# Value products in plain F32 in two 64-column array tiles, and latent scores with keys on partitions and the shift as a contraction row

## The chip, the core and the metric

The kernel runs on one core of a Trainium2 chip. The metric is the device time of one execution in microseconds; the profiled execution is one such execution with every instruction's start and duration recorded.

## What is computed

One layer of a hybrid trunk over 1024 latent tokens and 256 context tokens, width 1024, all in F32: half a SwiGLU step, then two attentions beside each other on one normalised input, their gated merge, and another half SwiGLU step. The change lies in the two attentions, both with 8 heads and values of width 64:

```python
# neighbourhood attention, by row of the 64-wide grid and block of 16 columns
s_loc = einsum('bjqhd,bjakhd->bhjqak', q_r, k_b) + bias; s_loc = where(valid, s_loc, neg)
s_ctx = einsum('bjqhd,bkhd->bhjqk', q_r, k_ctx)
p = softmax(concatenate([s_loc, s_ctx], -1), -1)
o_na = einsum(p_loc, v_b) + einsum(p_ctx, v_ctx)
# multi-head latent attention: 96 query/key dimensions, 1024 + 256 keys
s = einsum('bqhd,bkhd->bhqk', q * 96 ** -0.5, k)
o_mla = einsum('bhqk,bkhd->bqhd', softmax(s, -1), v)
```

## The kernel before

F32 products are made from FP32R halves: an operand x is split into hi (x rounded to FP32R) and lo (the rest), and `mm3` adds hi·hi, hi·lo and lo·hi. Nearly all of TensorE's work is such matmuls. The attentions lie between about 1342 and 1746 us of the profiled execution.

Neighbourhood attention has 32 items, one for each head and block of 16 columns, with 256 queries in two sets of 128. For each set the scores of 384 local keys and 256 context keys stand with queries on partitions; VectorE adds the bias and takes the row maximum (L1817), copies the context scores with their maximum (L1792), and ScalarE takes exp with the negated maximum as bias and the row sum beside it (L1826). Then TensorE transposes the weights 128x128 at a time (`turned`, L157), ScalarE casts them from PSUM to FP32R (L1850) and VectorE subtracts to get the rest (L1851). `weigh` multiplies each with a value tile of 128 columns, of which 64 are the values' hi and 64 their lo, so that two matmuls of 256 columns give all four products; the two halves are added afterwards. Six value blocks an item are twelve such matmuls.

Latent attention has 32 items of 256 queries, four for each head. `MlaItem.scores` makes scores of 1024 latent and 256 context keys for two sets of 128 queries, queries on partitions, again with three FP32R matmuls. The rest is as above: copy with maximum, exp (L1928), reciprocal of the sum (L1932), then five parts, each with four transposes, a cast (L1954), a subtraction (L1955) and four value matmuls of 256 columns.

`head_out` ends an item of both: it adds the two halves (ScalarE copies L1764 to L1768, VectorE L1769), multiplies with the reciprocal of the row sum (GpSimd L1770), and writes hi and lo of the result (L1772, L1773). The reciprocals come by `wide`: GpSimd spreads the sums over 128 columns (L1784) and TensorE transposes that, a pair for every two items.

The order is written out by hand: inside these stages `pin` keeps every instruction in program order on its engine. While item n is weighed, the scores of item n + 3 are made (`AHEAD`), value products run two parts late (`LAG`), and exp and sums are dealt out from the list `soft`. A matmul's records carry the helper's line (`mmul` L154, `turn_` L157, engine helpers L120, loads L132), so they are told apart by tiles: PSUM banks `bs` (scores, three), `bm` (transposes, three) and `bv` (outputs, two); `w` are weight tiles with queries, keys and values, `xu` and `t` work tiles, `st` small statistics, `xo` the outputs. Loads and stores all go through SyncE's queue (SP). The last items of latent attention are filled with `FirstMerge`, the first products of the merge.

Of the kernel before, what the change touches and what calls it, by code (L numbers as in the profile page):

```python
# [15 lines left out]
P = 128  # L16
# [27 lines left out]
def hybrid_block(ctx: ExitStack, tc: tile.TileContext, a: dict, out: bass.AP):  # L44
# [31 lines left out]
    def T2(dt=F32, n=512):  # L76
        return pools["t"].tile([P, n], dt, tag="t", name=nm("t"))

# [1295 lines left out]
    vws = [DR([NH, P, 512]) for _ in range(4)]  # L1374
    vcs = DR([NH, P, 256])
# [53 lines left out]
    def va_tile(s, t):  # L1429
        pb = s.product(t)  # L1430
        v = U(F32R)
        vv = v.rearrange("p (h c) -> p h c", h=NH)
        pv = pb.rearrange("p (h c) -> p h c", h=NH)
        split_to(vv[:, :, 0:64], vv[:, :, 64:128], pv)
        if t < 8:
            for j in range(4):
                for r in range(2):
                    row = 2 * t + r
                    o, q = 64 * r + KSTART[j], (row % 4) * 32
                    g = (row // 4) * P  # L1440
                    store(vws[j][:, q:q + 32, g:g + P].rearrange("h p c -> p h c"),
                          f32(v[o:o + 32, :]).rearrange("p (h c) -> p h c", h=NH))
        else:
            g = (t - 8) * P
            store(vcs[:, :, g:g + P].rearrange("h p c -> p h c"), f32(v).rearrange("p (h c) -> p h c", h=NH))
# [76 lines left out]
    vs = DR([NLAT + NCTX, D])  # L1522
# [46 lines left out]
    class NaHead:  # L1569


        def loads(self, h):
# [11 lines left out]
            self.bias = [U() if h == 1 else W(F32)]  # L1584
            ld(self.bias[0][:, :768], a["bias"][h, 0])
            yield
            if h == 1:
                self.second_bias()
                yield
            self.va = va = W()  # L1590
            for j in range(2):
                self.values(va, j)
            yield
            ld(f32(kvc[:, 256:512]), vcs[h])
            if h != 1:
                self.second_bias()
            yield
            if h == 0:
                self.third_bias()
                yield  # L1600
            self.vb = vb = W()
            for j in range(2, 4):
                self.values(vb, j)
            yield
            if h:
                self.third_bias()
                yield

        def second_bias(self):
            self.bias.append(W(F32))  # L1610
            ld(self.bias[1][:, :768], a["bias"][self.h, 1])

        def third_bias(self):
            self.bias.append(U(F32, "y") if self.h else W(F32))
            ld(self.bias[2][:, :768], a["bias"][self.h, 2])

        def values(self, v, j):
            o = (j % 2) * 512
            ld(f32(v[:, o:o + 512]), vws[j][self.h])
# [33 lines left out]
    def kv_heads(ci, cn):  # L1653
# [8 lines left out]
        for i, t in enumerate(tiles_of(ci)):  # L1662
            v = U(F32R)
# [707 lines left out]
```

## Time and profile before

| | |
|---|---|
| median of 3 runs | 2550.99 us (2550.88 to 2553.09) |
| span of the profiled execution | 2549.3 us |
| TensorE matmul busy | 2524.4 us, 99% |
| TensorE weight loads busy | 2156.4 us, 85% |
| VectorE busy | 1936.7 us, 76% |
| ScalarE busy | 1259.6 us, 49% |
| GpSimd busy | 214.1 us, 8% |
| neighbourhood attention, 1342 to 1480 us | PE 135.50, VectorE 128.13, ScalarE 120.16, GpSimd 61.59 us busy |
| latent attention, 1480 to 1746 us | PE 264.24, VectorE 221.09, ScalarE 210.21, GpSimd 68.96 us busy |

PE is TensorE's matmuls, PEld its weight loads, DVE is VectorE, ACT ScalarE, POOL GpSimd. Matmuls are pipelined, so the time of one is read from start to start and not from its own duration. A row of groups reads: line, engine, operation, output<-input tiles, shapes, count, then busy time and mean duration in ns, then idle time before and what ended it.

### The profile page before, as it was taken

How to read it: one execution, taken by the hardware profiler on the slowest of the kernel's cores; microseconds unless marked ns; L12 is line 12 of the kernel's file. 1: busy time of each engine (PE TensorE's matmuls, PEld its weight loads, DVE VectorE, ACT ScalarE, POOL GpSimd, SP SyncE). 2: the span in 40 equal slices, each digit the busy share in tenths (PEclk: the TensorE clock that was granted, in tenths of full speed). 3: DMA queues.
4: the chain of work that ended last, by engine and by line, in shares of the span. 5: the costliest groups of instructions: out<-in, count | busy, mean ns of one | idle time of the engine just before them, and what ended most of it. 6: DMA issues, size and time to landing. Idle time of an engine off the chain costs nothing.

```text
span 2549.3 us, 38224 instructions
## 1 busy us (share of the span) xinstructions
PE 2524.4 (99%) x13416; PEld 2156.4 (85%) x13416; DVE 1936.7 (76%) x3629; ACT 1259.6 (49%) x2375; POOL 214.1 (8%) x372
## 2 busy tenths in 40 slices
PE   8999999999999999999999999999999999999998
PEld 6888888888998888889889999998888888888887
DVE  4789986887786577874568988887886888766777
ACT  6632223446654753433448987783366323233444
POOL 1000000001000000001003522221021000000002
PEclk9999999999999999999999999999999999999999
DMA  8555543943674666755978733206845445326724
GB/s 308 162 174 196 192 153 116 346 137 132 230 271 141 211 235 221 244 180 179 297 292 289 236 92 75 65 13 245 320 135 201 160 158 166 112 99 239 269 71 165
DMA packets 245760, 479.47 MB, mean 188 GB/s; under 512 B 30464, under 2 KB 71616, under 8 KB 245568
## 3 DMA queue, kind: packets, MB, share of 16 engines
q1 hardware_dynamic: 245568, 477.02, 55.6%
q8 instruction: 106, 1.74, 0.3%
q14 instruction: 86, 0.70, 0.1%
HBM read 348.93 MB, written 127.99 MB: 187 GB/s over the span
## 4 chain that ended last, share of the span: by engine, by line
PE 85%; ACT 6%; DVE 6%; issue 3%; DMA 1%; POOL 0%; SPq 0%; DVEq 0%; POOLq 0%; ACTq 0%
PE bs L154 36%; PE bm L154 27%; PE bv L154 19%; PE bm L157 2%; ACT xu L1928 2%; DVE xu L1792 2%; DVE t L1955 1%; ACT t L1954 1%; ACT t L120 1%; PE bs L157 1%; DVE xv L120 1%; DVE xu L120 1%; ACT t L1928 1%; ACT t L1768 0%; ACT xu L120 0%
## 5 line engine op out<-in xcount | busy, mean ns | idle before, releaser
L120 ACT CAST xu<-t 128x512 fp32r<-128x512 f32 (+1 forms) x270 | 160.9, 601 | 494.2 <-DVE t L120 352.3
L154 PE MATMUL bm<-xu,xu 128*128 128x512 f32 (+2 forms) x1572 | 366.6, 386 | 0.0
L154 PE MATMUL bs<-xv,xu 128*128 128x512 f32 x1488 | 357.3, 389 | 0.3 <-DVE t L120 0.3
L154 PEld LDWEIGHTS bm<-xu,xu 128*128 128x128 f32 x1572 | 288.1, 188 | 56.7 <-ACT t L120 0.2
L154 PE MATMUL bv<-xv,xu 128*128 128x512 f32 x1342 | 335.4, 389 | 0.0
L154 PEld LDWEIGHTS bs<-xv,xu 128*128 128x128 f32 x1488 | 279.1, 188 | 59.0 <-issue 1.1
L154 PEld LDWEIGHTS bv<-xv,xu 128*128 128x128 f32 x1342 | 251.8, 188 | 52.2
L154 PE MATMUL bs<-xv,xv 128*128 128x512 f32 x1086 | 265.8, 390 | 0.0
L120 DVE TENSOR_TENSOR xu<-xu,xu 128x512 fp32r<-128x512 f32 (+1 forms) x296 | 202.2, 688 | 54.0 <-ACT xu L120 53.6
L154 PEld LDWEIGHTS bs<-xv,xv 128*128 128x128 f32 x1086 | 203.0, 188 | 41.7
L154 PE MATMUL bs<-xu,xu 128*128 128x512 f32 (+1 forms) x972 | 226.2, 382 | 0.0
L120 DVE TENSOR_TENSOR t<-t,t 128x512 f32<-128x512 f32 (+2 forms) x278 | 185.3, 674 | 45.2 <-ACT t L120 36.1
L154 PE MATMUL bs<-w,w 96*128 96x512 f32 (+3 forms) x832 | 206.1, 366 | 1.6 <-DVE st L1817 1.3
L154 PEld LDWEIGHTS bs<-xu,xu 128*128 128x128 f32 x972 | 177.4, 188 | 35.7 <-issue 1.4
L120 ACT CAST xv<-t 128x512 fp32r<-128x512 f32 x170 | 105.8, 622 | 167.4 <-PE bm L154 69.3
L120 POOL TENSOR_SCALAR st<-st 128x1 f32<-128x1 f32 (+1 forms) x66 | 29.7, 450 | 1884.8 <-ACT t L120 1866.7
L120 DVE TENSOR_TENSOR xu<-t,xu 128x512 fp32r<-128x512 f32 (+1 forms) x270 | 179.3, 664 | 10.7 <-ACT xu L120 10.6
L154 PE MATMUL bm<-xv,xv 128*128 128x512 f32 x690 | 182.9, 390 | 0.0
L120 ACT CAST xu<-xu 128x512 fp32r<-128x512 f32 x218 | 132.6, 618 | 70.2 <-DMA xu<-in_wo 46.8
L120 DVE TENSOR_TENSOR xv<-t,xv 128x512 fp32r<-128x512 f32 x170 | 117.1, 689 | 65.5 <-ACT xv L120 65.1
L154 PE MATMUL bv<-t,w 128*128 128x256 f32 x896 | 150.0, 288 | 2.5 <-DVE t L1955 1.6
L154 PEld LDWEIGHTS bm<-xv,xv 128*128 128x128 f32 x690 | 129.2, 188 | 27.0 <-issue 0.4
(246 smaller groups left out, 4228.1 us busy)
## 6 DMA issues: line engine op xcount, KB each, us to landing
d<-t SPq DMA_DIRECT2D x366, 256.0 KB, 2.7
t<-d SPq DMA_DIRECT2D x274, 256.0 KB, 3.7
xu<-in_f1w SPq DMA_DIRECT2D x59, 512.0 KB, 4.2
xu<-in_f2w SPq DMA_DIRECT2D x58, 512.0 KB, 3.8
t<-in_wada SPq DMA_DIRECT2D x112, 256.0 KB, 5.0
xv<-in_f1w SPq DMA_DIRECT2D x44, 512.0 KB, 6.8
xu<-in_winT SPq DMA_DIRECT2D x38, 512.0 KB, 5.2
w<-d SPq DMA_DIRECT2D x32, 512.0 KB, 6.6
```

The source lines that it names most:

```text
L120: return lambda *x, **y: pin(f(*x, **y))
L154: return pin(nc.tensor.matmul(o, s, m, start=start, stop=stop, skip_group_check=open_group[0]))
L157: return pin(nc.tensor.transpose(o, x, i))
L1792: nc.vector.tensor_scalar(dst, src, 1.0, FMIN, op0=ALU.mult, op1=ALU.max, accum_out=m)
L1928: nc.scalar.activation(x, x, AF.Exp, bias=n_[:, s:s + 1], accum_out=l[:, i:i + 1])
L1954: nc.scalar.copy(t[0], pb)
L1955: nc.vector.tensor_tensor(t[1], pb, f32(t[0]), op=ALU.subtract)
```

## The change

**Value products.** Values and weights stay plain F32 and are not split. `weigh` now makes two matmuls: values of 64 columns stand once in the left and once in the right 64 columns of the array, each with its own half of the queries, and the output fills 128 PSUM partitions. In the neighbourhood items the two sets of queries are the two tiles, 128 columns each; an item's transposed weights are copied out of PSUM once (two copies on ScalarE, one on VectorE) and its five pairs of products are collected and run together (`NaItem.weigh`). `NaPair` holds the output of two items and ends both together.

**Latent attention.** It has 16 items of 512 queries. `maxima` makes hi·hi scores with queries on partitions, ten blocks ("top") an item, only for the maximum. `shift` takes their maximum and negates it on VectorE; `row` transposes it to a row and writes it by four DMAs into partition 96 of the queries' tile, against a row of ones in the keys' tile. `scores` then makes scores with keys on partitions, for a block of 128 keys and 512 queries, in three matmuls of which the first contracts 97 rows, and exp goes from PSUM straight into the weights (`X`, a tile of five blocks). There are no transposes of weights. The row sums come from GpSimd's additions of blocks 0 to 4 (`add`), VectorE's reduction over blocks 5 to 9 and an addition (`total`), and a matmul with ones that sums over partitions and spreads the sum; `out` takes the reciprocal of 128x256 in PSUM and the product. `follow` sets the order: of item i's ten key blocks, the first half is weighed after the seventh, the second half and the ones after the third block of the next item, and the output follows two blocks later.

Loads and stores of values halve, since no lo is kept.

Diff, cut to its core; the bodies that fall away are in the listing above:

```diff
+    def X():
+        return pools["x"].tile([P, 2560], F32, tag="x", name=nm("xp"))
...
     def va_tile(s, t):
         pb = s.product(t)
-        v = U(F32R)
-        vv = v.rearrange("p (h c) -> p h c", h=NH)
-        pv = pb.rearrange("p (h c) -> p h c", h=NH)
-        split_to(vv[:, :, 0:64], vv[:, :, 64:128], pv)
+        v = U()[:, :512]
+        act.copy(v, pb)
...
-    def head_out(pv, n, h, hi, lo, shape):
...
-        x = sums[n // 2].rearrange("p (x i o) -> p i x o", i=2, o=1).to_broadcast([P, 2, 2, 64])
-        nc.gpsimd.tensor_copy(wide(n).rearrange("p (i x c) -> p i x c", i=2, x=2), x)
+        x = sums[n // 2].rearrange("p (x o) -> p x o", o=1).to_broadcast([P, 4, 64])
+        nc.gpsimd.tensor_copy(wide(n).rearrange("p (x c) -> p x c", x=4), x)
...
+    def weigh(pv, c, vts, pts, start, stop):
+        open_group[0] = True
+        for e in range(2):
+            n = pts[e].shape[-1]
+            mmul(pv[64 * e:64 * e + 64, c:c + n], vts[e], pts[e], start, stop)
+        open_group[0] = False
...
-    def weigh(pv, vtile, pt, start, stop):
-        mmul(pv[:, :256], vtile, pt[0], start=start, stop=False)
-        mmul(pv[:, :256], vtile, pt[1], start=False, stop=stop)
...
+        def out(self, n, h, j):
+            pv, t = self.pv[0], T2()
+            rb, o = t[:, 0:256], t[:, 256:512]
+            for i in range(2):
+                turn_(pv[:, 256 + i * P:256 + (i + 1) * P], wide(n)[:, i * P:(i + 1) * P], ident)
+            nc.scalar.copy(rb, pv[:, 256:512])
+            for x in range(len(self.pv)):
+                c = slice(x * P, x * P + 256 // len(self.pv))
...
+        def weigh(self, last=True):
+            pv = na_pairs[self.n // 2].bank(self.n)
+            for i, (vts, t) in enumerate(self.jobs):
+                weigh(pv, (self.n % 2) * P, vts, (t[:, 0:P], t[:, P:2 * P]), not self.begun, last and i == len(self.jobs) - 1)
+                self.begun = True
+            self.jobs = []
...
-                nc.scalar.copy(oh, src)
-                nc.vector.tensor_tensor(ol, src, f32(oh), op=ALU.subtract)
+                (nc.scalar.copy if eng else nc.vector.tensor_copy)(t[:, :n], pb[:, :n])
...
+        def maxima(self):
+            hd = self.hd
+            self.m, self.mc = m, mc = ST(8), ST(4)
+            q = lambda t: hd.qh[:QK, self.c0 + t * P:self.c0 + (t + 1) * P]
+            def top(d, c, pb):
+                nc.vector.tensor_reduce(d[:, c:c + pb.shape[-2]], pb, axis=AX.X, op=ALU.max)
+            for t in range(4):
                 for e in range(2):
...
+                    pb = PB("m")
+                    mmul(pb, q(t), hd.kh[:QK, e * 512:(e + 1) * 512], True, True)
+                    top(m, 2 * t + e, pb.rearrange("p (o c) -> p o c", o=1))
+                    yield
+                if t % 2:
+                    pb = PB("m")
                     for x in range(2):
...
+                        mmul(pb[:, x * 256:(x + 1) * 256], q(t - 1 + x), hd.kvc[:QK, 0:256], True, True)
+                    top(mc, t - 1, pb.rearrange("p (o c) -> p o c", o=2))
+                    yield
+        def shift(self):
+            n_, u = ST(4), ST(4)
+            nc.vector.tensor_reduce(u, self.m.rearrange("p (t e) -> p t e", t=4), axis=AX.X, op=ALU.max)
+            nc.vector.tensor_tensor(u, u, self.mc, op=ALU.max)
+            nc.vector.tensor_scalar(n_, u, -1.0, None, op0=ALU.mult)
+            self.n_ = n_
+        def row(self):
+            pt = PB("m")
+            turn_(pt[:4, :P], self.n_, ident)
+            rows = kr.rearrange("p a b -> p (a b)")[0:4, (self.i % 2) * P:(self.i % 2) * P + P]
+            nc.vector.tensor_copy(rows, pt[:4, :P])
+            for t in range(4):
+                put(f32(self.hd.qh[QK:QK + 1, self.c0 + t * P:self.c0 + (t + 1) * P]), rows[t:t + 1, :])
+        def scores(self, kb):
+            hd, c = self.hd, slice(self.c0, self.c0 + 512)
+            hi, lo = hd.key(0, kb), hd.key(1, kb)
+            pb = PB("s")
+            mmul(pb, hi[:QK + 1, :], hd.qh[:QK + 1, c], True, False)
+            mmul(pb, hi[:QK, :], hd.ql[:QK, c], False, False)
+            mmul(pb, lo[:QK, :], hd.qh[:QK, c], False, True)
+            if kb % 5 == 0:
+                self.pt[kb // 5] = X()
+            nc.scalar.activation(self.part(kb), pb, AF.Exp)
+        def part(self, kb):
+            return self.pt[kb // 5][:, (kb % 5) * 512:(kb % 5) * 512 + 512]
+        def add(self, kb):
+            if kb == 1:
+                self.acc = T2()
+            nc.gpsimd.tensor_tensor(self.acc, self.part(0) if kb == 1 else self.acc, self.part(kb), op=ALU.add)
+        def total(self):
+            self.l = T2()
+            nc.vector.tensor_reduce(self.l, self.pt[1].rearrange("p (k q) -> p q k", k=5), axis=AX.X, op=ALU.add)
+            nc.vector.tensor_tensor(self.l, self.l, self.acc, op=ALU.add)
+        def weigh(self, half):
+            if half == 0:
+                self.pv = PB("v")
+            for kb in range(5 * half, 5 * half + 5):
+                v = self.hd.v[:, kb * 64:(kb + 1) * 64]
+                x = self.part(kb)
+                weigh(self.pv, 0, (v, v), (x[:, 0:256], x[:, 256:512]), kb == 0, kb == 9)
+            if half:
+                v = ones.to_broadcast([P, 64])
+                weigh(self.pv, 256, (v, v), (self.l[:, 0:256], self.l[:, 256:512]), True, True)
+        def out(self):
+            t, h, pv = T2(), self.hd.h, self.pv
+            rb, o = t[:, 0:256], t[:, 256:512]
+            nc.vector.reciprocal(rb, pv[:, 256:512])
+            nc.vector.tensor_tensor(o, pv[:, 0:256], rb, op=ALU.mult)
+            def views(s):
+                hi, lo = [x[:, self.c0 + s * 256:self.c0 + s * 256 + 256] for x in omla[h // 2]]
+                return hi, lo, lambda x: x
+            heads_out(o, rb, (h % 2) * 64, views)
...
+    def follow(i, kb):
+        prev = mla[i - 1] if i else None
+        item = mla[i] if i < len(mla) else None
+        after = mla[i + 1] if i + 1 < len(mla) else None
+        if kb == 0 and prev:
+            prev.total()
+        if kb == 0 and i % 2 == 0 and i // 2 + 1 < NH:
+            mla_heads[i // 2 + 1].second()
+        if kb == 2 and prev:
+            prev.weigh(1)
+        if kb == 4 and prev:
+            prev.out()
+        if item and 1 <= kb < 6:
+            item.add(kb) if kb < 5 else None
+        if after and kb == 5:
+            after.shift()
+        if kb == 5 and i % 2 and i // 2 + 2 < NH:
+            mla_heads[i // 2 + 2].first()
+        if after and kb == 6:
+            after.row()
+        if item and kb == 6:
+            item.weigh(0)
+    for i, item in enumerate(mla):
+        for kb in range(10):
+            item.scores(kb)
+            next(tops, None)
+            if i == 0:
+                finish_one()
+                if pending and kb % 2 == 0:
+                    ending += pending.pop(0)
+            follow(i, kb)
...
```

In the orders below each row is an instruction: line, operation, output<-inputs and shape, then the engines whose work it waits for. First TensorE in the middle of the latent attention, before: scores of one item (`bs`), value products of an earlier one (`bv`) and transposes (`bm`) take turns, part by part.

```order
L157 MATMUL bm_18104<-ident,t_17652 128x128 [waits PE_49]
L157 MATMUL bm_18104<-ident,t_17652 128x128 x3
L154 MATMUL bs_18116<-w_17997,w_17995 128x512 [waits DVE_49]
L154 MATMUL bs_18116<-w_17998,w_17995 128x512
L154 MATMUL bs_18116<-w_17997,w_17996 128x512
L154 MATMUL bv_18080<-t_18070,w_17509 128x256 [waits Activation_49]
L154 MATMUL bv_18080<-t_18071,w_17509 128x256 [waits DVE_49]
L154 MATMUL bv_18080<-t_18070,w_17509 128x256
L154 MATMUL bv_18080<-t_18071,w_17509 128x256
```

And now, at the seventh key block of an item: a score block, a top block (`bm` from `w`), the transpose of the shift (`bm` from `ident` and `st`), and the first half of the value products as one burst.

```order
L157 MATMUL bs_3246_16099<-w_3106_15493,w_3107_15494 128x512 [waits Activation_49]
L157 MATMUL bs_3246_16099<-w_3109_15496,w_3107_15494 128x512
L157 MATMUL bs_3246_16099<-w_3106_15493,w_3124_15572 128x512
L157 MATMUL bm_3247_16104<-w_3175_15789,w_3174_15788 128x512 [waits DVE_49]
L160 MATMUL bm_3248_16107<-ident_76,st_3240_16078 4x128 [waits DVE_49,PE_49]
L157 MATMUL bv_3249_16114<-xp_3222_16001,w_3125_15573 64x256 x8
L157 MATMUL bv_3249_16114<-xp_3222_16001,w_3125_15573 64x256 [waits Activation_49]
L157 MATMUL bv_3249_16114<-xp_3222_16001,w_3125_15573 64x256
L157 MATMUL bs_3250_16125<-w_3106_15493,w_3107_15494 128x512
```

The transposes of weights are gone from between the scores, the value products stand together, and a transpose that waits for VectorE's shift has come in ahead of them. On VectorE a stretch of a latent item, before: copies with maximum from `bs`, subtractions from `bm`, and the small sums.

```order
L1955 TENSOR_TENSOR t_16111<-bm_16105,t_16110 128x512 [waits Activation_49]
L1792 TENSOR_SCALAR xu_16061,st_16056<-bs_16135 128x512 [waits PE_49]
L1955 TENSOR_TENSOR t_16131<-bm_16125,t_16130 128x512 [waits Activation_49]
L1931 TENSOR_TENSOR st_15804<-st_15924 128x2
L1955 TENSOR_TENSOR t_16150<-bm_16144,t_16149 128x512 [waits Activation_49,Pool_49]
L1932 RECIPROCAL st_15804<-st_15804 128x2 [waits DVE_49]
L1792 TENSOR_SCALAR xu_16061,st_16056<-bs_16156 128x512 [waits PE_49]
L1924 TENSOR_REDUCE st_16057<-st_16056 128x2 [waits DVE_49]
```

And now, in two pieces, first from the total of the item before to its reciprocal (`st` from `bm` are top reductions).

```order
L1993 TENSOR_REDUCE t_16749<-xp_16661 128x512 [waits Activation_49]
L1938 TENSOR_REDUCE st_16663<-bm_16746 128x1 [waits PE_49]
L1994 TENSOR_TENSOR t_16749<-t_16749,t_16607 128x512 [waits DVE_49,Pool_49]
L1938 TENSOR_REDUCE st_16663<-bm_16762 128x1 [waits PE_49]
L1938 TENSOR_REDUCE st_16663<-bm_16772 128x1 [waits PE_49]
L2010 RECIPROCAL t_16806<-bv_16704 128x256 [waits PE_49]
```

The subtractions and copies are gone; the total and the reciprocal stand among the top reductions. The second piece of the same engine, two top reductions later, goes from the product to the copy of the row.

```order
L2011 TENSOR_TENSOR t_16806<-bv_16704,t_16806 128x256 [waits DVE_49]
L1938 TENSOR_REDUCE st_16821<-bm_16823 128x1 [waits PE_49]
L1957 TENSOR_REDUCE st_16827<-st_16663 128x4 [waits DVE_49]
L1938 TENSOR_REDUCE st_16821<-bm_16836 128x1 [waits PE_49]
L1958 TENSOR_TENSOR st_16827<-st_16827,st_16664 128x4 [waits DVE_49]
L1959 TENSOR_SCALAR st_16826<-st_16827 128x4 [waits DVE_49]
L1966 COPY kr<-bm_16839 4x128 [waits DMAHW6_49,DMAHW1_49,DMAHW7_49,DMAHW0_49,PE_49]
```

A 128x512 reduction (the total), a 128x256 reciprocal and ten top reductions have taken the place of the subtractions and the copies with maximum; one top reduction (the seventh's) stands between the first and the second step of the shift. Third, TensorE in the neighbourhood attention, before: two value blocks of four matmuls, with transposes and scores between.

```order
L154 MATMUL bv_14928<-t_14839,w_14560 128x256
L154 MATMUL bv_14928<-t_14840,w_14560 128x256
L154 MATMUL bv_14928<-t_14839,w_14560 128x256
L154 MATMUL bv_14928<-t_14840,w_14560 128x256
L157 MATMUL bm_14935<-ident,xu_14711 128x128
L157 MATMUL bm_14935<-ident,xu_14712 128x128
L157 MATMUL bm_14935<-ident,xu_14711 128x128
L157 MATMUL bm_14935<-ident,xu_14712 128x128
L154 MATMUL bs_14943<-w_14851,w_14849 128x256
```

And now, where an item's value products come after the scores and ahead of the last two transposes:

```order
L157 MATMUL bs_13978<-w_13775,w_13769 128x384 [waits DVE_49]
L157 MATMUL bs_13978<-w_13775,w_13770 128x384
L157 MATMUL bv_13934<-t_13897,w_13527 64x128 [waits DMAHW3_49]
L157 MATMUL bv_13934<-t_13897,w_13527 64x128 x3
L157 MATMUL bv_13934<-t_13917,w_13519 64x128 x4
L157 MATMUL bv_13934<-t_13945,w_13527 64x128 [waits Activation_49]
L157 MATMUL bv_13934<-t_13945,w_13527 64x128
L160 MATMUL bm_13998<-ident,xp_13790 128x128 [waits PE_49]
L160 MATMUL bm_13998<-ident,xp_13790 128x128
```

Three groups of four matmuls between transposes and scores have become one burst of ten.

More of the change, by code (lines that the diff above doesn't have):

```diff
@@ L1750, in weights @@
         open_pool("w", "weights", 16, "left")
[L1752 to L1775 removed]
+    sums = {}
     def wide(n):
@@ L1798, in hybrid_block @@
+    na_pairs = [NaPair() for _ in range(NH * 2)]
     class NaItem:
```

336 lines of the change are left out of this document (142 added, 194 removed).

## The prediction

> **What bounds the kernel now.** I read the busy times first, then the chain that ended last.
>
> ```profile
> span 2549.3 us, 38224 instructions
> PE 2524.4 (99%) x13416; PEld 2156.4 (85%) x13416; DVE 1936.7 (76%) x3629; ACT 1259.6 (49%) x2375; POOL 214.1 (8%) x372
> PE 85%; ACT 6%; DVE 6%; issue 3%; DMA 1%; POOL 0%; SPq 0%; DVEq 0%; POOLq 0%; ACTq 0%
> ```
>
> TensorE is busy 99% and carries 85% of the chain, so what the change takes from TensorE's stream is gain and what makes TensorE wait is loss. The profiled execution spans 2549.3 us, 1.7 us under the median of 2550.99; I carry the differences over to the median. Then the stretches of the change, by windows (busy time of each engine, then granted clock, DMA share and GB/s):
>
> ```profile
> 1300.00:1342.00 42.00, 42.00 (x246) 37.03 (x245) 23.09 (x66) 15.13 (x28) 0.99 (x5) 1.00 0.68 247
> 1420.00:1460.00 40.00, 39.84 (x318) 39.26 (x317) 39.07 (x142) 37.84 (x93) 20.93 (x36) 1.00 0.75 222
> 1480.00:1746.00 266.00, 264.24 (x1870) 243.11 (x1869) 221.09 (x640) 210.21 (x471) 68.96 (x118) 1.00 0.24 61
> ```
>
> The neighbourhood attention (the middle row, typical of 1342 to 1480) has PE, VectorE and ScalarE all nearly full; the latent attention (the last row) has PE full at 99% and VectorE at 83%. The clock is whole. Now one latent item of 256 queries, by the timeline of PE (start, duration of the group, count):
>
> ```profile
> 1600.08 0.60 PE L157 MATMUL bm<-ident,xu 128*128 128x128 f32 x4
> 1600.44 0.94 PE L154 MATMUL bs<-w,w 96*128 96x512 f32 x3
> 1601.22 0.64 PE L154 MATMUL bv<-t,w 128*128 128x256 f32 x4
> 1601.70 0.60 PE L157 MATMUL bm<-ident,t 128*128 128x128 f32 x4
> ...
> 1606.57 0.38 PE L157 MATMUL bv<-ident,rope 128*128 128x128 f32 x2
> ...
> 1608.40 0.60 PE L157 MATMUL bm<-ident,xu 128*128 128x128 f32 x4
> ```
>
> A part is four transposes (0.36 from start to start), three score matmuls (0.78) and four value matmuls (0.48). Five parts take 1608.40 − 1600.08 = 8.32 us, that is 16.64 us for 512 queries; nothing stands idle between them. Only starts count: a matmul's own duration overlaps the next.
>
> **The prices of what is added.** A plain F32 matmul shows as two passes; the trace has such matmuls already, in four 32-column tiles that run side by side:
>
> ```profile
> 41.81 1.82 PE L154 MATMUL bv<-xv,sc 128*32 128x128 f32 x60
> 806.17 1.29 PE L154 MATMUL bv<-t,xu 128*128 128x512 f32 x5
> 807.40 1.07 PE L154 MATMUL bm<-t,strip 128*32 128x256 f32 x16
> 808.40 0.98 PE L154 MATMUL bv<-t,xu 128*128 128x512 f32 x3
> 1300.66 3.56 PE L154 MATMUL bm<-xu,xu 128*128 128x512 f32 x15
> L154 PE MATMUL bv<-xv,sc x256: 272/273/423, 10.7 to 43.4; 128*32 128x128 f32 x128
> L154 PE MATMUL bv<-t,w 128*128 128x256 f32 x429 | 71.5, 285 | 1.0 <-DVE t L1955 0.9
> L154 PE MATMUL bs<-xv,xu 128*128 128x512 f32 x1488 | 357.3, 389 | 0.3 <-DVE t L120 0.3
> L157 PEld LDWEIGHTS bv<-ident,rope x64: 137/141/143, 1354.2 to 1737.8; 128*128 128x128 f32 x64
> ```
>
> 60 records in four tiles are 15 passes of 128 columns: (1.82 − 0.27)/14 = 0.11 us a pass, so 0.22 for 256 columns, the four tiles sharing it. An ordinary 512-column matmul starts every (3.56 − 0.39)/14 = 0.23, one of 256 every (0.64 − 0.28)/3 = 0.12 (the four at 1601.22). The burst at 807.40 costs more than its four passes: the five before it need 4 x 0.23 = 0.92 to their last start, and 1.23 pass until the burst, 0.08 over a normal 0.23; the burst lasts 1.00 against 0.88; the three behind it have starts (0.98 − 0.39)/2 = 0.295 apart, 0.13 lost. I price a change of tile shape and back at 0.33 us. The Trainium skill ("TensorEngine Tiling (Array Packing)", Key Properties) says that changing the tiling mode drains TensorE; these rows agree.
>
> **The latent attention, 16 items of 512 queries.** Removed for each: 40 transposes, 40 value matmuls, one pair of wide transposes. Added: ten "top" blocks of hi·hi scores for the maxima (8 of 512 columns, 4 of 256: 8 x 0.23 + 4 x 0.12 = 2.32), 10 x 3 score matmuls of 512 (6.90), one small transpose for the row (0.11), 20 value matmuls in two 64-column tiles, which are ten pairs of two passes (20 x 0.22 = 4.40), the sum by ones (0.44), and two bursts (0.66). Sum 14.83 against 16.64: −1.81 an item if TensorE never waits, −29 us over 16.
>
> But it will wait. In VectorE's order the reduction of the seventh top block stands between the shift's first and last steps, and TensorE turns the row right behind that top block's matmul. The durations, by groups of the latent stretch and of single tiles:
>
> ```profile
> L1792 DVE TENSOR_SCALAR_CACHE_REDUCE xu<-bs 128x512 f32<-128x512 f32 x87 | 57.5, 680 | 0.0
> L1931 DVE TENSOR_TENSOR st<-st 128x2 f32<-128x2 f32 x22 | 3.4, 153 | 0.0
> L1824 DVE TENSOR_REDUCE st<-st 128x2 f32<-128x4 f32 x16 | 2.4, 149 | 0.2
> L1932 DVE RECIPROCAL st<-st 128x2 f32<-128x2 f32 x21 | 3.3, 155 | 0.0
> L1769 DVE TENSOR_TENSOR t<-t,bv 64x256 f32<-64x256 f32 x22 | 9.2, 418 | 9.7 <-ACT t L1768 8.3
> L1954 ACT CAST t<-bm 128x512 fp32r<-128x512 f32 x109 | 61.1, 582 | 13.3 <-PE bm L157 12.8
> L1770 POOL TENSOR_TENSOR t<-t,t 64x256 f32<-64x256 f32 x11 | 8.0, 730 | 51.5 <-DVE t L1769 46.8 <-PE bs L154 4.7
> L120 DVE TENSOR_TENSOR mod<-bv,bada x18: 153/158/167, 17.3 to 1813.7; 128x8 f32<-128x8 f32 x10, 128x4 f32<-128x4 f32 x8
> ```
>
> The matmul's result is there 0.39 after its start, the reduction takes 0.68, two tiny steps 0.15 each, the weight load about 0.14: 1.51, less the matmul's own 0.23, is about 1.3 us of idle TensorE in each item. What stands behind it on TensorE is the first half's value burst and the next scores, so nothing fills it. 14.83 + 1.3 = 16.13, −0.5 an item, **−8 us**. Bounds: −29 without that wait, and above zero if VectorE falls further behind.
>
> That hangs on two VectorE operations that the trace lacks. (1) The reciprocal of 128x256 in PSUM. Lower bound: a 256-wide TENSOR_TENSOR, 0.42 us. Upper bound: the 4-element reduction took 149, so some 145 ns are fixed; if all that the 2-element reciprocal has beyond (155 − 145 = 10) is per element, that is 5 ns, 1.4 us. Between the reciprocal and the row stand four top reductions (0.68 at most), the product (0.42) and three tiny steps, 3.6 us, against four blocks of 0.92 = 3.7 on TensorE; with the 1.3 us of wait that is there anyhow, 1.4 us are covered. I take 0.9, the middle, and +2 us in all for top banks that come free later. The Trainium skill ("VectorE: DVE Perf Modes", First, the fixed hardware budget) has Reciprocal as an iterative divide with a repeat count of 8; worked out as an estimate, 256 x 8 cycles at 0.96 GHz are 2.1 us, 0.7 past the cover, and the sum would be some 11 us higher. No run here shows a wide one.
>
> (2) The total: a TENSOR_REDUCE over five blocks that reads 2560 elements with a stride of 2 KB. At one element for each 1.04 ns, or 2.7 us, it fits: TensorE reaches the ones matmul one top, three blocks and ten pair passes after the last score, 0.24 + 3 x 0.92 + 2.2 + 0.1 = 5.3 us; beside this reduction the way has the drain (0.39 − 0.23 = 0.16), the last exp (0.58), a top reduction and an addition (0.68 each), 2.1. So up to 3.2 us nothing is lost; each microsecond above costs 16. The nearest rows are the strided 4- and 8-element additions (mod): 3 ns for 4 more elements by their medians 155 and 158, 0.75 ns each, to (167 − 155)/4 = 3 ns each at the worst. That gives 2.1 to 7.8 us; I take 2.7, nearest to the medians, and keep the rest for a rival.
>
> Hidden: ten exp (10 x 0.58) fit ScalarE's 16; GpSimd's four additions of 128x512, at 2 x 0.73 the most, and eight output steps fit; should GpSimd be late, the total's second step waits next. Four row DMAs go on SP each item. They land in about the small loads' time, against 5.9 us from the row to the next item's first score:
>
> ```profile
> w<-d SPq DMA_DIRECT2D x16, 32.0 KB, 3.3
> ```
>
> They stand ahead of the next heads' loads on SP, whose due time is an item later. At the entry the first head's loads and tops come while the last neighbourhood items load, and the first row's DMAs stand behind the second head's: I add one such landing, **+3 us**, once (0 to +6, two).
>
> **The neighbourhood attention, 32 items.** Twelve FP32R value matmuls of 256 (12 x 0.12 = 1.44) become five pairs in two passes of 128 columns (5 x 2 x 0.11 = 1.10), plus a burst at 0.25, less than 0.33 since a transpose's columns, not 512, are behind it; scores, transposes and the wide pair stay. That is −0.09 an item, and up to −0.2 if the last waits go too (PE 39.84 of 40), since VectorE's three subtractions an item become one copy: **−4 us** (−3 to −6). Value-tile subtractions and half the stores leave 1300 to 1342, where PE is 42.00 of 42.00 busy: 0.
>
> **Sum.** −8 − 4 + 3 + 2 = −7: 2551 − 7 = **2544 us**.
>
> **The rivals.** A (slower): the strided total reads slower than one element a cycle. It decides from 3.2 us on. At 3 ns an element (7.8 us) the ones matmul waits 4.6 us, +74: 2618; at half rate (5.4 us) 2.2 us, +35: 2579; at 4.1 us 2558. Against it the 0.75 ns of the mod rows; for it that those read PSUM and so few elements that fixed cost hides a rate. The Trainium skill ("SBUF — State Buffer", Specifications (TRN2)) says that 16-byte lines need two hits each for full bandwidth and that every crossing to a new line pays; by that this reduction, one hit a line, is slow. No row here bears on it in SBUF.
>
> B (no faster, or slower): the two 64-column tiles do not run side by side, or the pairs take two turns. Then 4.84 more a latent item and 1.1 a neighbourhood item, 77 + 35: 2656. The x60 row, where four tiles share a pass, speaks against it.
>
> C (faster): the wait at the row is not there, because top reductions run ahead of TensorE, or the four-way alternation of before costs more than I took off. −20 instead of −8: 2532, at best 2523.
>
> **How the numbers follow.** About 0.2%, ±5 us (2546 to 2556), is what a measurement of this kernel can tell from no change. My forecast 0.47 (own range 2534 to 2556: faster 0.30, same 0.16, slower 0.01); A 0.38 (same 0.04, slower 0.34); B 0.05, slower; C 0.10, faster. Together faster 0.40, same 0.20, slower 0.40. The range 2528 to 2597 leaves out B, the slow end of A (0.07) and half of C, about 0.17.
>
> **What would show it.** Idle TensorE of about 1.3 us an item before the row's transpose, released by VectorE's shift; none before the ones matmul. The total's reduction at 2.7 us and the reciprocal under 1.7. Two records of each pair 7 ns apart, passes of 0.22. Sixteen items in about 258 us. Wrong: a long wait of PE on VectorE at the ones matmul (A), passes twice as dense (B), or a latent item under 15.5 us (C).

## The result, and the profile after

| kernel | median us | to before, 95% interval |
|---|---|---|
| before | 2551.07 (2550.88 to 2553.09) | |
| changed | 2594.01 (2589.93 to 2595.56) | 1.0164 (1.0149 to 1.0178) |

The change costs 43 us, where the forecast was a gain of 7 (2544 us). The stated range holds the time only because it was drawn to take in rival A. The lines of the page of the changed kernel, as shown before the change:

```profile
span 2593.8 us, 36835 instructions
PE 2521.7 (97%) x13176; PEld 2073.4 (80%) x13176; DVE 1893.2 (73%) x3146; ACT 1121.3 (43%) x2007; POOL 255.3 (10%) x368
PE 87%; DVE 9%; ACT 2%; issue 1%; DMA 1%; SPq 0%; POOL 0%; POOLq 0%; DVEq 0%; ACTq 0%
PE bs L157 37%; PE bm L157 27%; PE bv L157 20%; DVE t L1993 3%; DVE st L1938 2%; PE bm L160 2%; DVE t L2010 1%; PE bs L160 1%; ACT t L123 1%; DVE xv L123 1%; DVE xu L123 1%; ACT xu L123 0%; DVE t L1994 0%; DVE t L123 0%; PE bv L160 0%
```

TensorE was 99% busy and is 97%; on the chain VectorE has grown from 6 to 9%, with two new lines, the total (L1993) and the reciprocal (L2010). The windows of the two attentions (busy times, then the granted clock) tell where:

```profile
1420.00:1460.00 40.00, 39.26 (x396) 33.73 (x394) 29.28 (x119) 30.89 (x75) 15.81 (x31) 1.00 0.64 179
1500.00:1700.00 200.00, 165.78 (x881) 110.50 (x881) 146.05 (x187) 64.38 (x112) 81.87 (x95) 0.94 0.22 53
```

In the latent attention TensorE is idle 34 of 200 us, and its clock, whole before, is 0.94 in the mean. Cut into windows of 0.25 us, the clock is not a little lower everywhere: it is half in twelve stretches of about 3.4 us each (eleven behind the entry), and whole between them. The inner 3 us of one:

```profile
1580.25:1583.25 3.00, 3.00 (x16) 1.46 (x12) 0.00 (x0) 0.00 (x0) 1.46 (x3) 0.50 0.01 1
```

One item on TensorE's timeline (the bracket is the idle time before, and what ended it):

```profile
1573.14 0.65 PE L157 MATMUL bv<-t,strip 128*64 128x256 f32 x4 [1.51 <-DVE t L1994]
1573.73 0.97 PE L157 MATMUL bs<-w,w 97*128 97x512 f32 x3
...
1577.34 0.40 PE L157 MATMUL bm<-w,w 96*128 96x512 f32 x1
1579.30 0.27 PE L160 MATMUL bm<-ident,st 128*4 128x128 f32 x1 [1.56 <-DVE st L1959]
1579.50 4.05 PE L157 MATMUL bv<-xp,w 128*64 128x256 f32 x20
1583.48 0.73 PE L157 MATMUL bs<-w,w 97*128 97x512 f32 x2
```

There are two waits, at the ones matmul for the total and at the row for the shift. From start to start they cost 1.66 us (1.88 from the last value matmul, against a pass of 0.22) and 1.73 (1.96 from the last top block, against a 512-column matmul's 0.23). From item to item the idle time at the row changes between 1.4 and 2.0 us behind the entry; the sums of both waits follow with `e1_unit`. Behind the second the burst of 20 records takes 4.05 us; with the clock whole it takes 2.38 (below). The two operations that the profile before did not have, and the shift's last step, each by its line (duration ns minimum, median, maximum):

```profile
L1993 DVE TENSOR_REDUCE t<-xp x16: 4680/4718/4729, 1489.8 to 1780.2; 128x512 f32<-128x2560 f32 x16
L2010 DVE RECIPROCAL t<-bv x16: 1744/1748/1758, 1496.8 to 1786.4; 128x256 f32<-128x256 f32 x16
L1959 DVE TENSOR_SCALAR st<-st x16: 154/356/614, 1468.2 to 1758.2; 128x4 f32<-128x4 f32 x16
```

From the first total to the last, an item of 512 queries takes (1780.2 − 1489.8)/15 = 19.36 us in the mean, against 16.64 before: 2.72 x 16 = 43.5 us, as much as the whole loss.

### The profile page after: what moved, and what is told of

Its sections match the earlier page's. It is cut to its first block, busy times and chain, and to the rows that moved or that the text cites. A ratio compares the mean times of both kernels' runs of the same rounds, so it can differ in the third digit from the quotient of the medians.

```text
span 2593.8 us, 36835 instructions
## 1 busy us (share of the span) xinstructions
PE 2521.7 (97%) x13176; PEld 2073.4 (80%) x13176; DVE 1893.2 (73%) x3146; ACT 1121.3 (43%) x2007; POOL 255.3 (10%) x368
## 4 chain that ended last, share of the span: by engine, by line
PE 87%; DVE 9%; ACT 2%; issue 1%; DMA 1%; SPq 0%; POOL 0%; POOLq 0%; DVEq 0%; ACTq 0%
PE bs L157 37%; PE bm L157 27%; PE bv L157 20%; DVE t L1993 3%; DVE st L1938 2%; PE bm L160 2%; DVE t L2010 1%; PE bs L160 1%; ACT t L123 1%; DVE xv L123 1%; DVE xu L123 1%; ACT xu L123 0%; DVE t L1994 0%; DVE t L123 0%; PE bv L160 0%
## 5 line engine op out<-in xcount | busy, mean ns | idle before, releaser
L157 PE MATMUL bs<-w,w 96*128 96x512 f32 (+1 forms) x736 | 197.0, 384 | 1.9 <-DMA w<-kr 1.3
L1979 ACT ACTIVATE xp<-bs 128x512 f32<-128x512 f32 x160 | 95.5, 597 | 205.1 <-PE bs L157 204.5
L1938 DVE TENSOR_REDUCE st<-bm 128x1 f32<-128x512 f32 (+1 forms) x160 | 105.7, 679 | 74.3 <-PE bm L157 74.3
```

The source lines that it names most:

```text
L157: return pin(nc.tensor.matmul(o, s, m, start=start, stop=stop, skip_group_check=open_group[0]))
L1938: nc.vector.tensor_reduce(d[:, c:c + pb.shape[-2]], pb, axis=AX.X, op=ALU.max)
L1979: nc.scalar.activation(self.part(kb), pb, AF.Exp)
```

## The experiments

First the stride, the clock, the late VectorE steps together, and the neighbourhood part by itself. Beside these runs the kernel before measured 2551.9 to 2553.0 us, so times from different sessions compare to about 2 us. `e1_unit`:

```diff
-            nc.vector.tensor_reduce(self.l, self.pt[1].rearrange("p (k q) -> p q k", k=5), axis=AX.X, op=ALU.add)
-            nc.vector.tensor_tensor(self.l, self.l, self.acc, op=ALU.add)
+            nc.vector.tensor_reduce(self.l, self.pt[1].rearrange("p (q k) -> p q k", k=5), axis=AX.X, op=ALU.add)
+            nc.vector.scalar_tensor_tensor(self.l, self.l, 1.0, self.acc, op0=ALU.add, op1=ALU.add)
```

> The changed kernel, with one edit: the total's reduction takes the same 2560 elements five and five in a row, so it reads with unit stride instead of a stride of 2 KB (its sums are then not the row sums; the addition behind it adds 1 so that nothing is divided by zero). Theory (the stride is what makes the reduction slow): it takes 2.7 us instead of 4.72, the 1.7 us that TensorE waits at the ones matmul goes, -27 us over 16 items, and some or all of the twelve half-clock windows with it, up to -20 more: 2547 to 2567 us. Rival (a reduction to 512 outputs is slow at any stride): it still takes 4.7 us, and the time stays at 2594 within 5.

Measured 2566.92 us, 27 less than the changed kernel, at the upper end of what was expected. The waits at the ones and at the row (us in total, times, longest), first two lines the changed kernel, then `e1_unit` with its total and the addition behind it:

```profile
PE bv L157 <- DVE t L1994: 23.0, 15, 1.8
PE bm L160 <- DVE st L1959: 24.9, 15, 2.0
PE bv L157 <- DVE t L1994: 7.9, 15, 0.9
PE bm L160 <- DVE st L1959: 25.0, 15, 2.0
L1993 DVE TENSOR_REDUCE t<-xp x16: 2807/2808/2821, 1487.6 to 1751.7; 128x512 f32<-128x2560 f32 x16
L1994 DVE SCALAR_TENSOR_TENSOR t<-t,t x16: 693/1556/1687, 1491.0 to 1754.6; 128x512 f32<-128x512 f32 x16
```

The same reduction takes 2.81 us at unit stride and 4.72 at 2 KB: 1.10 and 1.84 ns an element. The stride is the cause. The wait at the ones falls by 15 us but is not gone, the one at the row is untouched, and the latent windows' clock is 0.97: four half-clock stretches instead of twelve, to which the rest of the 27 us falls. What is left at the ones is not the reduction: the addition behind it (L1994) takes 1.56 us by its median, and took 0.68 in the changed kernel. In the six items from 1560 to 1660 us it ends some 0.55 us after an addition of GpSimd that started before it, which `e10_best` and `e13_gps` come back to.

`e4_fill` puts matmuls nobody reads into the waits:

```diff
             pt = PB("m")
+            for _ in range(8):
+                mmul(pt[:, P:512], self.hd.kh[:QK, 0:P], self.hd.kh[:QK, 0:384], True, True)
             turn_(pt[:4, :P], self.n_, ident)
...
             if half:
+                for _ in range(8):
+                    mmul(self.pv[:, 256:512], self.hd.kh[:QK, 0:P], self.hd.kh[:QK, 0:256], True, True)
                 v = ones.to_broadcast([P, 64])
```

> The changed kernel with work added and nothing else: eight idle matmuls of 384 columns (1.4 us) ahead of the row's transpose and eight of 256 columns (1.0 us) ahead of the ones matmuls, into PSUM columns that are not read, where TensorE waits 1.7 us in each place. Theory (the waits themselves let TensorE's clock fall to half): the half-clock windows go, 12 x 1.7 = 20 us: about 2574 us, faster with more work. Rival (the clock falls because of the plain F32 column tiles, or for another reason that the waits do not set): the windows stay at about twelve and the time at 2594, or above.

Measured 2580.78 us: 256 matmuls more, and 13 us faster. The window of the latent attention:

```profile
1500.00:1700.00 200.00, 193.43 (x1121) 140.09 (x1119) 155.56 (x196) 69.07 (x120) 87.45 (x100) 1.00 0.23 57
```

The clock is whole, with the same column tiles. So the waits take the clock down, and this costs time beside the waits themselves. From row to row thirteen items take 18.5 us each, and 19.7 in the changed kernel, so about 1.2 us an item. The whole gains less than the 20 that I had counted, since the second row, where there were only 0.6 us to wait, comes 1.6 us later behind the added matmuls; 13 us is what is left after their cost.

`e5_all` adds the blocks one by one, moves `out` behind the row and the shift ahead:

```diff
-            nc.vector.tensor_reduce(self.l, self.pt[1].rearrange("p (k q) -> p q k", k=5), axis=AX.X, op=ALU.add)
+            nc.vector.tensor_tensor(self.l, self.l, self.part(9), op=ALU.add)
             nc.vector.tensor_tensor(self.l, self.l, self.acc, op=ALU.add)
+
+        def add_late(self, kb):
+            if kb == 6:
+                self.l = T2()
+            nc.vector.tensor_tensor(self.l, self.part(5) if kb == 6 else self.l, self.part(kb), op=ALU.add)
...
+        if after and kb == 4:
+            after.shift()
         if kb == 2 and prev:
             prev.weigh(1)
-        if kb == 4 and prev:
-            prev.out()
...
-        if after and kb == 5:
-            after.shift()
...
+        if kb == 7 and prev:
+            prev.out()
+        if item and kb >= 7:
+            item.add_late(kb - 1)
```

> The changed kernel with both late VectorE steps mended: blocks 5 to 8 are added one by one behind their exp and block 9 and the rest at the end (additions of 128x512, 0.6 us each, instead of the one strided reduction), the reciprocal and the product come after the row's transpose (eighth key block instead of fifth), and the shift one key block earlier. Theory (both waits are VectorE's lateness, the clock follows them): 14.96 us an item of 512 queries, as TensorE's own work adds up to: 2594 - 28 (row) - 27 (ones) - 20 (clock) = 2519, 2515 to 2530 us. Rival (VectorE is too full, the waits move to the top banks or the output): 2540 us or more.

Measured 2548.28 us, 0.9981 (0.9971 to 0.9991): better, but 29 us above the expectation. The ones wait is gone, the row's is not. VectorE's timeline shows why:

```profile
1560.60 1.76 DVE L2014 RECIPROCAL t<-bv 128x256 f32<-128x256 f32 x1 [0.76 <-PE bv L157]
1562.27 1.22 DVE L1938 TENSOR_REDUCE st<-bm 128x1 f32<-128x512 f32 x2
1563.41 0.15 DVE L1957 TENSOR_REDUCE st<-st 128x4 f32<-128x8 f32 x1
1563.57 0.69 DVE L1938 TENSOR_REDUCE st<-bm 128x1 f32<-128x512 f32 x1
1564.18 0.70 DVE L1958 TENSOR_TENSOR st<-st,st 128x4 f32<-128x4 f32 x1
1564.81 0.68 DVE L1938 TENSOR_REDUCE st<-bm 128x1 f32<-128x512 f32 x1
1565.41 0.49 DVE L1959 TENSOR_SCALAR st<-st 128x4 f32<-128x4 f32 x1
```

These instructions are not pinned, so the scheduler still put the reciprocal ahead and a top reduction into each gap of the shift: its three steps, which can take as little as 0.15 us each (the first one here; L1959's shortest above), take 2.5 from the first start to the last end. Moving a call in the code had moved less than I thought.

`e6_na` is the kernel before with the edits to `va_tile`, `NaHead` and `NaItem`, `NaPair`, `heads_out` and the tiled `weigh` alone.

> The kernel before with the neighbourhood attention's part of the change alone (values unsplit, plain F32 pairs in two 64-column tiles, two items ended together); latent attention as before. Theory: the 0.22 us an item that the profile of the changed kernel shows (3.97 against 4.19 from reciprocal to reciprocal), -7 us: 2544 us. Rival (that was an artefact of what overlaps it at its end): 2551 within 2.

Measured 2546.43 us, 0.9977 (0.9967 to 0.9986): −6 us, close to the 7 that were expected. The neighbourhood part is a gain, all the loss is the latent part's.

Then VectorE's order. `vec` instead of `nc.vector` keeps an instruction in the written order; `e7_pin` does that to tops, shift, row copy and output of `e5_all`, `e8_shift` to tops and shift of the changed kernel alone, `e9_order` is `e7_pin` with the strided total.

```diff
-            nc.vector.tensor_reduce(u, self.m.rearrange("p (t e) -> p t e", t=4), axis=AX.X, op=ALU.max)
+            vec.tensor_reduce(u, self.m.rearrange("p (t e) -> p t e", t=4), axis=AX.X, op=ALU.max)
```

> The changed kernel with VectorE's order alone mended at one place: the three steps of the shift stand together, with the seventh top reduction behind them instead of between them. Theory (that reduction, 0.61, is part of the row's wait of 1.73 us): the wait falls to about 1.1, -10 us, and the clock windows stay or get fewer, up to -10 more: 2574 to 2586 us. Rival (the wait is the reciprocal's 1.75 us, and the order of the steps makes nothing): 2594 within 4.

Measured 2577.19 us, 17 less than the changed kernel, as expected: the steps' order is part of the row's wait. Its sum is 18 us in the latent part, against 25 with the old order; the rest I put down to the clock (0.97 in the mean from 1500 to 1700, instead of 0.94). The wait at the ones is as it was:

```profile
PE bm L160 <- DVE st L123: 18.1, 15, 1.6
PE bv L157 <- DVE t L1994: 23.0, 15, 1.8
```

> The changed kernel with the output late, the shift early and VectorE's written order as in the first of these, but with the strided total of 4.72 us left in. Theory (two separate waits): no wait at the row, -28 us, the wait at the ones matmul stays at 1.7 us or a little more, and with a single wait the clock falls less often: 2546 to 2566 us. Rival (one wait takes the place of the other): the ones wait grows by what the row saves, 2590 us.

> The kernel of the run before (additions instead of the strided reduction, output late, shift early), and now VectorE keeps the written order: the three steps of the shift stand together right behind the tenth top reduction, and the reciprocal behind the row's copy. Theory (the row's wait, 1.97 and 1.63 us by turns there, was reductions and a reciprocal put ahead of the shift's steps): no wait at the row, no half-clock window: 2548 - 16 x 1.55 - 4 x 1.7 = 2517, 2510 to 2524 us. Rival (the row's own way over PSUM, a copy and four DMAs is too long, or the top banks come free too late): 2535 us or more, with a wait before the first scores of an item or before a top block.

Both expectations failed. `e9_order` took 2630.72 us and `e7_pin` 2575.29: the row's wait is 0.56 or nothing, but new ones are larger. In `e9_order`, VectorE, then TensorE:

```profile
1570.25 1.75 DVE L123 RECIPROCAL t<-bv 128x256 f32<-128x256 f32 x1
1571.92 4.56 DVE L1993 TENSOR_REDUCE t<-xp 128x512 f32<-128x2560 f32 x1
1577.46 0.79 PE L157 MATMUL bm<-w,w 96*128 96x512 f32 x1 [4.36 <-DVE st L123]
```

The total, still free to move, was put ahead of the last top reductions. All three top banks are full behind it, and TensorE waits 4.36 us for one. In `e7_pin`, by the same views:

```profile
1578.26 1.86 DVE L1998 TENSOR_TENSOR t<-t,xp 128x512 f32<-128x512 f32 x1
1580.64 2.30 DVE L1992 TENSOR_TENSOR t<-t,xp 128x512 f32<-128x512 f32 x1
1583.79 0.92 PE L157 MATMUL bv<-t,strip 128*64 128x256 f32 x4 [2.59 <-DVE t L1993]
```

Additions of 0.68 us take 1.9 and 2.3 in some places; with the reciprocal among them they end late for the ones. Each of these two ends 0.55 us after one of GpSimd's instructions.

The next three kernels try three places for these steps. `e10_best` takes the additions and the early shift of `e5_all`, pins all of VectorE's steps, writes the maxima negated, so that the separate negation falls away, and puts the output into the gap of the first value burst:

```diff
-                nc.vector.tensor_reduce(d[:, c:c + pb.shape[-2]], pb, axis=AX.X, op=ALU.max)
+                vec.tensor_reduce(d[:, c:c + pb.shape[-2]], pb, axis=AX.X, op=ALU.max, negate=pb.shape[-2] == 2)
...
-            nc.vector.tensor_reduce(u, self.m.rearrange("p (t e) -> p t e", t=4), axis=AX.X, op=ALU.max)
-            nc.vector.tensor_tensor(u, u, self.mc, op=ALU.max)
-            nc.vector.tensor_scalar(n_, u, -1.0, None, op0=ALU.mult)
+            vec.tensor_reduce(u, self.m.rearrange("p (t e) -> p t e", t=4), axis=AX.X, op=ALU.max, negate=True)
+            vec.tensor_tensor(n_, u, self.mc, op=ALU.min)
...
         if after and kb == 6:
             after.row()
+        if kb == 6 and prev:
+            prev.out()
```

`e11_ones` (strided total) and `e12_ones` (additions) move the ones matmuls (`close`) instead:

```diff
         if item and kb == 6:
+            if prev:
+                prev.close()
             item.weigh(0)
+        if item and prev and kb == 7:
+            prev.out()
```

> The changed kernel with VectorE in the written order, the total by additions, the shift in two steps (no separate negation) behind the tenth top reduction, and the reciprocal and product right behind the row's copy, where TensorE's first value burst (2.3 us) sends VectorE no top block. Theory (a step of VectorE costs where it stands ahead of what TensorE waits for, and nothing in VectorE's gaps): row wait under 0.3 us; from the burst to the ones matmul VectorE has six top reductions and six additions, 7.3 us, against 7.8 on TensorE, so little wait there, and a whole clock: about 15.3 us an item, 2551 - 7 - 21 = 2523, 2516 to 2535 us. Rival (additions with two operands in SBUF are held up by GpSimd's output steps, as single ones took 1.9 and 2.3 us in the run with the written order): 1 us and more at the ones matmul again, with half-clock windows: 2540 us or more.

> The changed kernel with the strided reduction left as it is, and the ones matmuls moved from the second to the first value burst of the next item, about 9 us later, the output one block behind that; VectorE in the written order, the shift early and in two steps. Theory (4.72 us cost only by their deadline): VectorE has 14.3 us of work in an item of 15, no wait at the ones; the top banks, held while the long reduction runs, cost TensorE about 1 us an item: 2551 - 7 - 11 = 2533, 2522 to 2548 us. Rival (one long instruction holds up every top reduction behind it, wherever its deadline is): 2 us or more an item before a top block, half-clock windows, 2555 us or more.

> As the one before (ones matmuls in the next item's first value burst, output behind it, written order), but with the total by additions. Theory: neither the total nor GpSimd's hold-ups have a near deadline, no instruction of VectorE is longer than the reciprocal's 1.75 us, and 12.3 of 15 us are used: TensorE's own 14.96 us an item, a whole clock: 2551 - 7 - 27 + 3 = 2520, 2513 to 2528 us. Rival (the reciprocal among the late top blocks delays them and the waits return at the top banks): 2535 us or more.

`e10_best` measured 2537.71 us, 0.9942 (0.9925 to 0.9959), between what was expected (to 2535) and its rival (from 2540); `e11_ones` 2593.74; `e12_ones` 2554.75, 1.0010 (1.0001 to 1.0019). In the last two the rivals came true, at the top banks:

```profile
1563.14 4.74 DVE L123 TENSOR_REDUCE t<-xp 128x512 f32<-128x2560 f32 x1
1569.96 0.80 PE L157 MATMUL bm<-w,w 96*128 96x256 f32 x2 [2.32 <-DVE st L123]
PE bm L157 <- DVE st L123: 19.9, 38, 0.7
```

The first two lines are `e11_ones`: with no deadline near, the long reduction still holds up the top reductions behind it, 2.3 us an item. The third is `e12_ones`, where the reciprocal and the held-up additions do it in small pieces. In `e10_best` the row's wait is gone, and one at the ones is left. VectorE's last two additions, GpSimd beside them, and TensorE:

```profile
1568.49 1.37 DVE L123 TENSOR_TENSOR t<-t,xp 128x512 f32<-128x512 f32 x1
1569.96 1.58 DVE L123 TENSOR_TENSOR t<-t,t 128x512 f32<-128x512 f32 x1
1568.03 1.27 POOL L1988 TENSOR_TENSOR t<-xp 128x512 f32<-128x512 f32 x1 [1.82 <-ACT xp L1978]
1569.39 1.60 POOL L1988 TENSOR_TENSOR t<-t,xp 128x512 f32<-128x512 f32 x1
1571.60 0.65 PE L157 MATMUL bv<-t,strip 128*64 128x256 f32 x4 [0.80 <-DVE t L123]
```

Each of the two runs some 0.55 us past the end of GpSimd's (1569.30, 1570.99), as if it worked only when GpSimd is done. GpSimd's additions are those of the next item, so neither waits for the other's result. `e13_gps` lets GpSimd run at another time (against `e10_best`):

```diff
-            if kb == 1:
+            if kb == 3:
                 self.acc = T2()
-            nc.gpsimd.tensor_tensor(self.acc, self.part(0) if kb == 1 else self.acc, self.part(kb), op=ALU.add)
+            nc.gpsimd.tensor_tensor(self.acc, self.part(2) if kb == 3 else self.acc, self.part(kb), op=ALU.add)
...
-            vec.tensor_tensor(self.l, self.part(5) if kb == 6 else self.l, self.part(kb), op=ALU.add)
+            vec.tensor_tensor(self.l, self.part(0) if kb == 6 else self.l, self.part(1 if kb == 6 else kb), op=ALU.add)
...
-        if item and 1 <= kb < 6:
-            item.add(kb) if kb < 5 else None
+        if item and 3 <= kb < 7:
+            item.add(kb)
```

> The best run so far (2537.7 us) with the same instructions on every engine and other data in two of them: GpSimd adds blocks 2 to 6 instead of 0 to 4, so its four additions run in key blocks 3 to 6 and not 1 to 4, and VectorE adds blocks 0 and 1 instead of 5 and 6. In the run before, VectorE's last two additions took 1.37 and 1.58 us instead of 0.68, each until a GpSimd addition of the next item ended, and TensorE waited 0.95 us at the ones matmul. Theory (VectorE's additions with two operands in SBUF stand still while GpSimd reads): with GpSimd out of the way those two take 0.68 and the wait at the ones goes: -0.95 x 14 = -13: 2524 us, 2520 to 2529. Rival (they waited for exp or for the sums, not for GpSimd): 2537 within 3.

Measured 2523.38 us, 0.9886 (0.9869 to 0.9902), as expected: 29 us faster than before, 71 than the change as it was made. VectorE's last two additions, TensorE from one row to the next, and the latent windows:

```profile
1594.22 0.68 DVE L123 TENSOR_TENSOR t<-t,xp 128x512 f32<-128x512 f32 x1
1595.00 0.69 DVE L123 TENSOR_TENSOR t<-t,t 128x512 f32<-128x512 f32 x1
1585.43 0.27 PE L160 MATMUL bm<-ident,st 128*4 128x128 f32 x1
1593.74 2.38 PE L157 MATMUL bv<-xp,w 128*64 128x256 f32 x20
1595.95 0.60 PE L157 MATMUL bv<-t,strip 128*64 128x256 f32 x4
1600.31 0.27 PE L160 MATMUL bm<-ident,st 128*4 128x128 f32 x1
1480.00:1720.00 240.00, 239.37 (x1394) 169.31 (x1393) 194.53 (x304) 101.13 (x177) 137.67 (x143) 1.00 0.27 69
```

No wait, a whole clock, 14.88 us an item (1600.31 − 1585.43).

## Why the prediction was wrong

The sum failed at VectorE's steps, not at TensorE's work: it had no wait at the ones matmul, too short a one at the row, and no term for the clock that falls with them.

- **TensorE's own work was right.** The sum was 14.83 us an item; where nothing waits it is 14.88. The pairs of tiles share their passes: ten pair passes in 2.38 us, the last one's drain included. Rival B is out.
- **The neighbourhood part was right**: −4 forecast (−3 to −6), −6 measured.
- **The total was mis-sized, and with it the wait at the ones was left out**, the step marked (2): 2.7 us taken, 4.72 measured. The slack of 3.2 us was right within 0.2 (4.72 less the wait of 1.66 is 3.06). The prediction's own price, 16 us for each above 3.2, gives +24; the wait at the ones measured 1.66 x 16 = 27. This is rival A, given 0.38, and `e1_unit` shows its mechanism. The mod rows, on which I leaned, read PSUM and are so short that a rate does not show in them; their line gives one median, 158 ns, for both shapes, and not the 155 and 158 that I used. The Trainium skill's rule of two hits on a 16-byte line ("SBUF — State Buffer", Specifications (TRN2)), which spoke against this step, is what the run agrees with: 1.84 ns an element against 1.10.
- **The reciprocal was mis-sized**, the step marked (1): 0.9 taken, 1.75 measured, past the bound of 1.4 from the 2-element row and past its cover, which was also 1.4. By the prediction's own cover the 0.35 above it make the row's wait 1.65 instead of 1.3; it is 1.73. No run changes the reciprocal alone; where it stands behind the row's copy, with the shift earlier and in the written order (`e7_pin`, `e9_order`), the row's wait is 0.56 or nothing.
- **The clock was put at nothing.** That it was whole before was read from a kernel without waits; two waits of 1.7 us in each item take it to 0.94. The eleven half-clock stretches between the first total and the last are 11 x 3.4/2 = 19 us; `e4_fill` gains 13 net of its own matmuls.
- Together: 19.36 us measured less 14.88 of work is 4.48, of which 1.66 are at the ones and 1.73 at the row; the 1.1 that are left go to the clock, near the 19/15 = 1.25 of the stretches and the 1.2 of `e4_fill`. Against 16.64 before, 16 items lose 43.5 us. Less the 6 of the neighbourhood part this is 37.5 of the 43; the 5 that are left lie at the entry, the end or outside, and were not taken apart. The prediction's own +3 and +2 for the entry and the top banks are as large.
- That the range held 2594 is luck. A's own price for a total of 4.72 us is 2544 + 24 = 2568; the other 26 came from the clock (1.1 x 16 = 18) and the row (0.43 x 16 = 7), which no rival had.
- The cover that let GpSimd's four additions and eight output steps fit counted GpSimd's time, and not that its reads and VectorE's exclude each other. In the changed kernel this cost nothing (L1994 takes 0.68 us); in `e1_unit`, `e7_pin` and `e10_best` it did.

## What to carry to other kernels

Where TensorE is the bound, sum its work and then ask of each wait which engine's queue it hangs on, in that engine's real order: one long instruction costs all that is queued behind it, and a short step costs wherever a scheduler puts it ahead of what TensorE waits for. A wait can also cost by the clock, so two small ones in each item are dearer than they look. An operation that the profile lacks, such as a strided reduction or a wide reciprocal, is measured before an order is built around it.

## What the hardware showed

- A TENSOR_REDUCE on VectorE reads F32 from SBUF at a stride of 2 KB at 1.84 ns an element, and in a row at 1.10 (2560 elements, 4.72 and 2.81 us).
- A RECIPROCAL of 128x256 from PSUM takes 1.75 us, 6.8 ns an element; a product of that shape takes 0.42.
- An addition on VectorE with both operands in SBUF takes 0.68 us alone and up to 2.3 beside GpSimd's work; it then ends some 0.55 us after GpSimd's instruction. Moving GpSimd's additions brought the last two of an item back to 0.68 (`e13_gps`); two earlier ones still take 1.1 there beside GpSimd's output steps. The Trainium skill ("SBUF — State Buffer", Who interferes with whom) says that such an instruction and a GpSimd one that reads SBUF exclude each other; the runs agree.
- TensorE's clock falls without a long pause: two waits of 1.7 us in each item of 19.4 give 0.94, one of about 1.4 in an item of 17 gives 0.97 (`e5_all`), one of 0.95 us an item gives 1.00 (`e10_best`). The Trainium skill ("TensorE: Matmul & The Clock Gate", Part 1: The HAM clock gate (the "warmup" mystery)) has the half rate after an idle window of about 3.4 us; in the changed kernel's latent part no single wait was longer than 2.0, and how much idle time it takes is not shown here.
